# Retention keys turned by VectorE and through DRAM, and a head's states and outputs placed one pair of products later

## The chip, the core and the metric

The kernel runs on one core of a Trainium2 chip. The metric is the device time of one execution in microseconds (us). Engines: PE is TensorE (PEld its weight loads), DVE is VectorE, ACT is ScalarE, POOL is GpSimd, SP is SyncE, which here only issues DMAs.

## The reference

One layer of a hybrid encoder on 512 tokens of width 2048. A projection of the normalized input is split into a sparse attention, a retention with 8 heads of width 128, and gates. The part that is changed is the retention's chunkwise form. Per head, with `rq` and `rk` rotated:

```python
scores = jnp.einsum('bnqhd,bnkhd->bnhqk', qc, kc) * intra_decay
intra = jnp.einsum('bnhqk,bnkhe->bnqhe', scores, vc)
kv = jnp.einsum('bnkhd,bnkhe->nbhde', kc * to_end[:, :, None], vc)
...
cross = jnp.einsum('bnqhd,nbhde->bnqhe', qc * from_start[:, :, None], prev)
y = (intra + cross).reshape(B, L, R_HEADS, R_VAL_DIM)
```

`kv` contracts over tokens, so the keys, which leave the projection with channels on partitions, are needed with tokens on partitions.

## The kernel before

The order of every engine's instructions is written out by hand. A clock of program steps (`step`, one for two matmuls in a pair of products) runs `later(n, f)` jobs n steps after they were asked for. What an engine does is in program order; it waits on semaphores where data or buffers are not ready.

`gemm_pair` computes two 128-column blocks of a projection with seven half-size products. Its 14 runs of 8 matmuls go to the banks v p v p q r q r p p v v p p, a run with `wh` (the high part of a weight) or with `wl` (the low part). It has seven units of weights, 0 to 6, from four loaded tiles `wraw`, called t, w11, w21 and w22 here. ACT makes `wh` from `wraw` (L156), DVE makes `wl` (L161). Unit 4 is tile t after POOL has added another block of weights to it with an accumulating DMA (`add_block`, L119), which POOL issues when DVE has made unit 0's `wl`. Unit 4's `wh` waits for the landing of that DMA. SP loads a pair's tiles (L132) while the pair before it is in the program, as buffers come free, in order.

Three pairs make one head of the retention: the pair of its queries and keys, and two pairs of gates, called **pair A** and **pair B** here. `rotate(1, ...)` is called when the first has ended, and the numbers in `steps` count from there: 0 to 56 lie in A, 56 to 112 in B, 112 to 168 in the next head's pair of queries and keys. Before, all matmuls of a head's retention lie in A: the scores at step 24 (L927) and right behind them three transposes of the keys on PE (L938, into `ps_t`), which ACT copies with the factor `dect[:, 256]` into `kn` (step 29, L941); the states `ps_kv` at 39 (L947), ACT's copy and DVE's recurrence of them (L950, L953), and the outputs `ps_y` at 51 (L962, L964). DVE then normalizes them, turns them in 32x32 blocks (`back`, L990), and SP places the blocks through four DMAs into DRAM (`yd`, L994). B ends with the first use of the next pair. `kn` is the stationary operand of `ps_kv`: PE loads it as weights.

Of the kernel before, what the change touches and what calls it, by code (L numbers as in the profile page):

```python
# [20 lines left out]
NH = 8  # L21
# [14 lines left out]
def block_kernel(tc, xT, pT, posb, posq, w_in, w_v, w_r0, w_r1, w_ik, w_a, w_b, w_o, w_ple, w_gate,  # L36
# [4 lines left out]
    with contextlib.ExitStack() as ctx:  # L41
# [10 lines left out]
        def U(name, dt=F32):  # L52
            return up.tile([128, L], dt, name=name, tag="u")
# [4 lines left out]
        def P(name):  # L58
            return pp.tile([128, L], F32, name=name, tag="p")
# [831 lines left out]

        yd, bd, zd, qd, kd = (dp.tile([NH, 128, L], F32, name=n) for n in ("yd", "bd", "zd", "qd", "kd"))
        vd = dp.tile([2, 7, 128, L], F32, name="vd")

        def retention(h):

            hc = slice(128 * (h % 4), 128 * (h % 4) + 128)
            g128 = (1.0 - 2.0 ** (-5.0 - h)) ** 128
            dect, rv = U("dect"), U("rvh")
            later(24, lambda: sp.dma_start(dect[:, 0:257], dec[:, h, :]))  # L900
            later(32, lambda: sp.dma_start(rv.rearrange("p (t c) -> p t c", t=NT),
                                           rd[h // 4, :, :, hc].rearrange("t p c -> p t c")))
            ct, st = R["ct"], R["st"]
            E = {}

            def rotate(i, o):
                E[i] = o
                b = U("rb")
                act.activation(b[0:64, :], o[64:128, :], AF.Copy)
                act.activation(b[64:128, :], o[0:64, :], AF.Copy)  # L910
                later(3, lambda: dve.tensor_mul(o, o, ct))
                later(5, lambda: dve.tensor_mul(b, b, st))
                later(7, lambda: dve.tensor_add(o, o, b))
                if i:
                    for n, f in steps:
                        later(n, f)

            def queries():
                E["qt"] = U("qt")
                dve.tensor_mul(E["qt"][:, 0:384].rearrange("p (t q) -> p t q", t=3),  # L920
                               E[0][:, 128:].rearrange("p (t q) -> p t q", t=3),
                               dect[:, None, 128:256].to_broadcast([128, 3, 128]))

            def scores():
                ps = E["ps"] = P("ps_rs")
                for t in range(NT):
                    pe.matmul(ps[:, tok(t)], E[1][:, tok(t)], E[0][:, tok(t)], start=True, stop=True)  # L927

            def decay():
                at = E["at"] = U("at")  # L930
                dve.tensor_mul(at.rearrange("p (t q) -> p t q", t=NT), E["ps"].rearrange("p (t q) -> p t q", t=NT),
                               dect[:, None, 0:128].to_broadcast([128, NT, 128]))

            def keys(i):
                if i == 0:
                    ps = E["pk"] = P("ps_t")
                    for t in range(3):
                        pe.transpose(ps[:, tok(t)], E[1][:, tok(t)], ident)  # L938
                else:
                    E["kn"] = U("kn")  # L940
                    act.activation(E["kn"][:, 0:384], E["pk"][:, 0:384], AF.Copy, scale=dect[:, 256:257])  # L941

            def states(i):
                if i == 0:
                    ps = E["ps"] = P("ps_kv")
                    for t in range(3):
                        pe.matmul(ps[:, tok(t)], E["kn"][:, tok(t)], rv[:, tok(t)], start=True, stop=True)  # L947
                elif i == 1:
                    E["s"] = U("state")
                    act.activation(E["s"][:, 0:128], E["ps"][:, 0:128], AF.Copy)  # L950
                else:
                    for t in (1, 2):
                        dve.scalar_tensor_tensor(E["s"][:, tok(t)], E["s"][:, tok(t - 1)], g128, E["ps"][:, tok(t)],  # L953
                                                 op0=OP.mult, op1=OP.add)

            def values_out(t):
                if t == 0:
                    E["py"] = P("ps_y")
                    E["st"] = S("gst", 24)
                    E["mv"] = S("gmv", 8)  # L960
                o = E["py"][:, tok(t)]
                pe.matmul(o, E["at"][:, tok(t)], rv[:, tok(t)], start=True, stop=(t == 0))  # L962
                if t:
                    pe.matmul(o, E["qt"][:, tok(t - 1)], E["s"][:, tok(t - 1)], start=False, stop=True)  # L964

            def norm():
                st, mv, py = E["st"], E["mv"], E["py"]
                for t in range(NT):
                    dve.bn_stats(st[:, 6 * t:6 * t + 6], py[:, tok(t)])
                for t in range(NT):  # L970
                    dve.bn_aggr(mv[:, 2 * t:2 * t + 2], st[:, 6 * t:6 * t + 6])
                rs = S("grs", 4)
                dve.tensor_scalar(rs, mv.rearrange("p (t c) -> p t c", c=2)[:, :, 1], EPS, None, op0=OP.add)
                pool.tensor_tensor(rs, rs, mhalf[:, 0:NT], op=OP.pow)
                E["rs"] = rs

            def scale():
                mv, rs = E["mv"], E["rs"]
                yn = U("yn")
                for t in range(NT):  # L980
                    dve.tensor_scalar(yn[:, tok(t)], E["py"][:, tok(t)], mv[:, 2 * t:2 * t + 1], rs[:, t:t + 1],
                                      op0=OP.subtract, op1=OP.mult)
                E["yn"] = yn

            def back(i):


                if i == 0:
                    E["yb"] = U("yb")
                    dve.transpose(out=E["yb"].rearrange("p (j t c) -> p t j c", j=4, t=4),  # L990
                                  in_=E["yn"].rearrange("p (t j c) -> p t j c", t=4, j=4))
                else:
                    i -= 1
                    sp.dma_start(yd[h].rearrange("(j r) (i x) -> i r j x", j=4, i=4)[i],  # L994
                                 E["yb"][32 * i:32 * i + 32, :].rearrange("r (j x) -> r j x", j=4))

            steps = [(9, queries), (24, scores), (24, lambda: keys(0)), (28, decay), (29, lambda: keys(1))]
            steps += [(n, lambda i=i: states(i)) for i, n in enumerate((39, 41, 43))]
            steps += [(51, lambda t=t: values_out(t)) for t in range(NT)]
            steps += [(57, norm), (70, scale), (90, lambda: back(0))]  # L1000
            steps += [(126 + 2 * i, lambda i=i: back(i)) for i in range(1, 5)]
            return rotate

        x_wanted = collections.deque(x_away)
# [627 lines left out]
X_AWAY = 4  # L1632
X_BACK = (4, 6, 8, 10, 12, 14, 22, 24, 26, 28, 30, 32)
HEAD = 13
WARM = 10
MANUAL = True

# [98 lines left out]
```

## Time and profile before

| | |
|---|---|
| time, median of 3 runs | 1652.87 us (1652.41 to 1652.98) |
| time of the profiled execution | 1653.05 us |
| its span, first to last instruction | 1651.3 us |
| PE busy | 1642.4 us, 99% of the span |
| DVE, ACT, POOL busy | 1310.3, 961.7, 232.7 us |
| chain that ended last, by engine | PE 96%, DVE 2%, ACT 1% |
| retention heads | scores of head 0 at 293.1 us, of head 7 at 726.8 us |

The profiled execution took 1.75 us more than its span, for what lies before the first and after the last instruction. The chain is the work that ended last, followed back from the end: a thing that isn't on it may become slower until it meets it.

### The profile page before, as it was taken

What the parts mean: (1) busy time and instruction counts of PE and PEld (TensorE: products, weight loads), DVE (VectorE), ACT (ScalarE), POOL (GpSimd) and SP (SyncE); (2) the same over time, 40 slices, a digit from 0 to 9 for tenths busy, and PEclk for the clock granted to TensorE, in tenths of its full rate; (3) what the DMA queues carried; (4) which work ended last, traced back from release to release, by engine and by line L of the source; (5) the groups of instructions that cost most, each with busy time, mean ns of one, the idle gap of its engine ahead of it and who ended that gap; (6) DMA issues with size and microseconds to landing.
All of it is one profiled execution on the core that took longest, in us unless ns stands there. A gap on an engine that the chain in (4) does not pass through costs nothing.

```text
span 1651.3 us, 25215 instructions
## 1 busy us (share of the span) xinstructions
PE 1642.4 (99%) x9302; PEld 1444.7 (87%) x9302; DVE 1310.3 (79%) x2030; ACT 961.7 (58%) x1481; POOL 232.7 (14%) x257
## 2 busy tenths in 40 slices
PE   9999999999999999999999999999999999999998
PEld 8998888888888888888888888888888888888997
DVE  8788879888988888877766766787768877888884
ACT  7556545555555555657777765566644444576653
POOL 3100112111111111112331122100000111100111
PEclk9999999999999999999999999999999999999999
DMA  8427999788788788789988888997566788765973
GB/s 311 118 88 236 323 260 277 193 208 223 192 209 216 191 209 220 195 206 248 259 230 228 214 234 219 244 386 272 178 205 180 188 220 226 206 216 146 246 234 134
DMA packets 132987, 362.70 MB, mean 220 GB/s; under 512 B 15936, under 2 KB 28736, under 8 KB 132864
## 3 DMA queue, kind: packets, MB, share of 16 engines
q1 hardware_dynamic: 92608, 239.78, 42.1%
q0 software_dynamic: 27440, 98.32, 32.1%
q10 hardware_dynamic: 12816, 23.00, 3.8%
q8 instruction: 73, 1.20, 0.3%
q14 instruction: 50, 0.41, 0.1%
HBM read 313.32 MB, written 47.71 MB: 219 GB/s over the span
## 4 chain that ended last, share of the span: by engine, by line
PE 96%; DVE 2%; ACT 1%; issue 0%; DVEq 0%; ACTq 0%
PE ps_p L326 26%; PE ps_v L326 17%; PE ps_q L326 9%; PE ps_r L326 9%; PE ps_w L233 3%; PE ps_w L232 3%; PE ps_w L234 3%; PE ps_vn L881 2%; PE ps_vn L879 2%; PE ps_vn L880 2%; PE ps_iq L234 1%; PE ps_iq L232 1%; PE ps_iq L233 1%; PE ps_pg L233 1%; PE ps_pg L232 1%; PE ps_pg L234 1%
## 5 line engine op out<-in xcount | busy, mean ns | idle before, releaser
L161 DVE TENSOR_TENSOR wl<-wraw,wh 128x1024 fp32r<-128x1024 f32 (+3 forms) x472 | 568.4, 1216 | 149.6 <-ACT wh L156 147.2
L156 ACT ACTIVATE wh<-wraw 128x1024 fp32r<-128x1024 f32 (+3 forms) x471 | 486.7, 1041 | 238.5 <-DVE wraw L163 114.6
L119 POOL DMA_DIRECT2D wraw<-w_in x120 | 106.3, 965 | 571.2 <-DVE wl L161 392.1
L326 PE MATMUL ps_p<-hs,wh 128*128 128x512 f32 x640 | 161.0, 393 | 0.0
L265 ACT ACTIVATE e<-ps_p 128x512 f32<-128x512 f32 x152 | 90.3, 594 | 117.3 <-PE ps_p L326 114.9
L326 PEld LDWEIGHTS ps_p<-hs,wh 128*128 128x128 f32 x640 | 115.0, 189 | 20.6
L326 PE MATMUL ps_p<-hs,wl 128*128 128x256 f32 x640 | 89.9, 283 | 0.0
L326 PEld LDWEIGHTS ps_p<-hs,wl 128*128 128x128 f32 x640 | 82.5, 192 | 0.1
L326 PE MATMUL ps_q<-ha,wh 128*128 128x512 f32 x320 | 80.8, 394 | 0.0
L326 PE MATMUL ps_v<-ha,wh 128*128 128x512 f32 x320 | 80.0, 392 | 0.0
L326 PE MATMUL ps_r<-hs,wh 128*128 128x512 f32 x320 | 79.0, 389 | 0.0
L326 PE MATMUL ps_v<-hs,wh 128*128 128x512 f32 x320 | 79.0, 389 | 0.0
L326 PE MATMUL ps_p<-ha,wh 128*128 128x512 f32 x320 | 79.0, 389 | 0.0
L800 ACT ACTIVATE mk<-relf,thr 128x512 f16<-128x512 f32 (+3 forms) x128 | 66.7, 555 | 16.5 <-DVE go L1101 12.0
L1101 DVE TENSOR_TENSOR go<-e_t 128x256 f32<-128x256 f32 x160 | 68.2, 426 | 6.1 <-issue 0.4
L326 PEld LDWEIGHTS ps_r<-hs,wh 128*128 128x128 f32 x320 | 60.1, 188 | 12.5
L326 PEld LDWEIGHTS ps_v<-hs,wh 128*128 128x128 f32 x320 | 60.1, 188 | 12.5
L326 PEld LDWEIGHTS ps_p<-ha,wh 128*128 128x128 f32 x320 | 60.1, 188 | 12.5
L119 POOL DMA_DIRECT2D wraw<-w_o x24 | 21.1, 938 | 348.6 <-DVE t L356 191.4
L326 PEld LDWEIGHTS ps_v<-ha,wh 128*128 128x128 f32 x320 | 59.5, 188 | 12.1
L269 DVE TENSOR_TENSOR e_t<-ps_p,pv 128x512 f32<-128x512 f32 x48 | 33.1, 690 | 45.4 <-ACT e L265 45.2
L326 PEld LDWEIGHTS ps_q<-ha,wh 128*128 128x128 f32 x320 | 57.5, 189 | 12.1 <-issue 1.3
(479 smaller groups left out, 3806.6 us busy)
## 6 DMA issues: line engine op xcount, KB each, us to landing
wraw<-w_in SPq DMA_DIRECT2D x170, 512.0 KB, 5.1
wraw<-w_in POOLq DMA_DIRECT2D x120, 512.0 KB, 8.2
wraw<-w_o SPq DMA_DIRECT2D x32, 512.0 KB, 5.0
wraw<-w_o POOLq DMA_DIRECT2D x24, 512.0 KB, 7.4
wraw<-w_gate SPq DMA_DIRECT2D x24, 512.0 KB, 4.9
wraw<-w_v SPq DMA_DIRECT2D x16, 512.0 KB, 8.7
wraw<-w_b SPq DMA_DIRECT2D x16, 512.0 KB, 5.6
wraw<-w_a SPq DMA_DIRECT2D x16, 512.0 KB, 3.8
```

The costliest lines, as they stand in the source:

```text
L119: pool.dma_start(out=view(raw_tiles[r], nk, cols), in_=src[:, k0:k0 + nk, :], accum_op=OP.add)
L156: act.activation(h, raw, AF.Copy)
L161: dve.tensor_sub(l, raw, h.bitcast(F32))
L232: pe.matmul(o, h[:, k, w], a, start=(s == order[0]), stop=False)
L233: pe.matmul(o, h[:, k, w], b, start=False, stop=False)
L234: pe.matmul(o, l[:, k, w], a, start=False, stop=(s == order[-1]))
L265: act.activation(E[n], src, AF.Copy)
L269: f(t, x, y)
L326: pe.matmul(o[:, co], w[:, k], src, start=(n < 4 and begin and k == 0 and j == 0), stop=(ended[n] == 16), skip_group_check=True)
L800: act.activation(bias_e[b][i // per][:, ln * (i % per):ln * (i % per + 1)], relf[:, :ln], AF.Sign, bias=thr[:, q:q + 1])
L879: pe.matmul(o, a[:, tok(t)], h[:, k], start=(s == 0), stop=False)
L1101: dve.tensor_add(o[:, q], c0, c1)
```

## The change

The three transposes on PE and their PSUM bank go. DVE turns the keys in 32x32 blocks into `kb` (step 29), SP sends them with four DMAs into a new DRAM tile `krd` (steps 32 to 33) and loads it back as `kr` (step 46), and ACT makes `kn` from `kr` at step 75, with the factor from a small copy `te`. The states move from steps 39, 41 and 43 to 77, 79 and 81, the outputs from 51 to 83, their normalization and turning with them. The head's values `rvh` are loaded at step 40, behind the sends, and no longer before pair A.

```diff
+        krd = dp.tile([NH, 128, 384], F32, name="krd")
+
+        def blocks(b, src, n):
+            w = 32 * n
+            dve.transpose(out=b[:, 0:4 * w].rearrange("p (j t c) -> p t j c", j=4, t=n),
+                          in_=src[:, 0:4 * w].rearrange("p (t j c) -> p t j c", t=n, j=4))
+
+        def send(dst, b, i):
+            sp.dma_start(dst.rearrange("(j r) (i x) -> i r j x", j=4, i=4)[i],
+                         b[32 * i:32 * i + 32, 0:dst.shape[1]].rearrange("r (j x) -> r j x", j=4))
...
-            later(32, lambda: sp.dma_start(rv.rearrange("p (t c) -> p t c", t=NT),
-                                           rd[h // 4, :, :, hc].rearrange("t p c -> p t c")))
...
+            def own_values():
+                rv = E["rv"] = U("rvh")
+                sp.dma_start(rv.rearrange("p (t c) -> p t c", t=NT), rd[h // 4, :, :, hc].rearrange("t p c -> p t c"))
...
+                E["te"] = S("tend", 4)[:, 0:1]
+                dve.tensor_copy(E["te"], dect[:, 256:257])
 
             def keys(i):
                 if i == 0:
-                    ps = E["pk"] = P("ps_t")
-                    for t in range(3):
-                        pe.transpose(ps[:, tok(t)], E[1][:, tok(t)], ident)
+                    E["kb"] = U("kb")
+                    blocks(E["kb"], E[1], 3)
+                elif i < 5:
+                    send(krd[h], E["kb"], i - 1)
+                elif i == 5:
+                    E["kr"] = U("kr")
+                    sp.dma_start(E["kr"][:, 0:384], krd[h])
                 else:
                     E["kn"] = U("kn")
-                    act.activation(E["kn"][:, 0:384], E["pk"][:, 0:384], AF.Copy, scale=dect[:, 256:257])
+                    act.activation(E["kn"][:, 0:384].rearrange("p (t i c) -> p i t c", t=3, i=4),
+                                   E["kr"][:, 0:384].rearrange("p (i t c) -> p i t c", i=4, t=3),
+                                   AF.Copy, scale=E["te"])
...
-            steps = [(9, queries), (24, scores), (24, lambda: keys(0)), (28, decay), (29, lambda: keys(1))]
-            steps += [(n, lambda i=i: states(i)) for i, n in enumerate((39, 41, 43))]
-            steps += [(51, lambda t=t: values_out(t)) for t in range(NT)]
-            steps += [(57, norm), (70, scale), (90, lambda: back(0))]
-            steps += [(126 + 2 * i, lambda i=i: back(i)) for i in range(1, 5)]
+            steps = [(9, queries), (24, scores), (28, decay), (40, own_values)]
+            steps += [(n, lambda i=i: keys(i)) for i, n in enumerate(KEYS_AT)]
+            steps += [(n, lambda i=i: states(i)) for i, n in enumerate(STATES_AT)]
+            steps += [(OUT_AT[0], lambda t=t: values_out(t)) for t in range(NT)]
+            steps += [(OUT_AT[1], norm), (OUT_AT[2], scale)]
+            steps += [(n, lambda i=i: back(i)) for i, n in enumerate(OUT_AT[3:])]
...
+KEYS_AT = (29, 32, 32, 33, 33, 46, 75)
+STATES_AT = (77, 79, 81)
+OUT_AT = (83, 87, 94, 105, 128, 130, 132, 134)
```

On ACT, before, `kn` of head 1 stands in pair A, between the `wh` of units 5 and 6 (`pv` and the `e` tiles are copies of finished PSUM banks):

```order
L265 ACTIVATE pv<-ps_v 128x512
L265 ACTIVATE e_3633<-ps_p 128x512
L156 ACTIVATE wh<-wraw 128x1024 x2
L941 ACTIVATE kn<-ps_t,dect 128x384
L156 ACTIVATE wh<-wraw 128x1024
```

After the change it stands in pair B:

```order
L265 ACTIVATE pv<-ps_v 128x512
L265 ACTIVATE e_3844<-ps_p 128x512
L156 ACTIVATE wh<-wraw 128x1024
L959 ACTIVATE kn<-kr,tend 128x4x3x32
L970 ACTIVATE state<-ps_kv 128x128
L156 ACTIVATE wh<-wraw 128x1024 x2
```

The `wh` just ahead of `kn` is that of unit 4 of pair B, and `kn` has moved behind it.

On SP, before, one head's DMAs stand in this order (the last tile of pair A, then the values, then the tiles of two and three quarters pairs, then the outputs):

```order
L900 DMA dect<-dec 128x257
L132 DMA wraw<-w_in 128x1024
L901 DMA rvh<-rd 128x4x128
L132 DMA wraw<-w_in 128x1024 x11
L994 DMA yd<-yb 32x4x128 x4
```

After it:

```order
L910 DMA dect<-dec 128x257
L132 DMA wraw<-w_in 128x1024 x5
L902 DMA krd<-kb 32x4x96 x4
L916 DMA rvh<-rd 128x4x128
L956 DMA kr<-krd 128x384
L132 DMA wraw<-w_in 128x1024 x7
L902 DMA yd<-yb 32x4x128 x4
```

The sends, the values and the load of `kr` now stand ahead of the tiles that are loaded in pair B's part of the program.

On DVE, before, pair A of head 1 goes on like this behind the scores' decay (`at`; MAX and MATCH_REPLACE are a round of the attention's top-k, which runs in the background):

```order
L931 TENSOR_TENSOR at<-ps_rs,dect 128x512
L161 TENSOR_TENSOR wl<-wraw,wh 128x1024
L776 MAX m_3692<-isc 128x8
L777 MATCH_REPLACE isc<-m_3692,isc 128x256
L161 TENSOR_TENSOR wl<-wraw,wh 128x1024 x2
L953 SCALAR_TENSOR_TENSOR state<-state,ps_kv 128x128 x2
```

After it:

```order
L943 TENSOR_TENSOR at<-ps_rs,dect 128x512
L946 COPY tend<-dect 128x1
L161 TENSOR_TENSOR wl<-wraw,wh 128x1024
L898 STREAM_TRANSPOSE kb<-go 128x3x4x32
L776 MAX m_3695<-isc 128x8
L777 MATCH_REPLACE isc<-m_3695,isc 128x256
L161 TENSOR_TENSOR wl<-wraw,wh 128x1024 x2
L269 TENSOR_TENSOR e_t<-ps_v,e_3726 128x512
```

The small copy and the turning of the keys have come ahead of the last `wl`, that of unit 0 of pair B, and the states have left.

## Rows read from the trace of the kernel before

**Rows 1.** The page's chain that ended last, by engine.

```profile
PE 96%; DVE 2%; ACT 1%; issue 0%; DVEq 0%; ACTq 0%
```

**Rows 2.** The chain in order of time, head 1, pair A: start us, us, what.

```profile
355.14 0.89 PE ps_rs L927 x8
356.03 0.33 PE ps_t L938 x3
...
360.82 0.67 PE ps_kv L947 x6
...
365.26 0.45 PE ps_y L962 x4
365.70 0.22 PE ps_y L964 x2
```

**Rows 3.** View by tile, whole span: count, duration ns min/median/max, first and last start.

```profile
L938 PE MATMUL ps_t<-cs,go x24: 272/273/273, 294.0 to 727.9; 128*128 128x128 f32 x24
L941 ACT ACTIVATE kn<-ps_t,dect x8: 557/564/566, 297.2 to 729.8; 128x384 f32<-128x384 f32 x8
L990 DVE STREAM_TRANSPOSE yb<-yn x8: 701/704/705, 322.0 to 755.1; 128x512 f32<-128x512 f32 x8
L973 DVE TENSOR_SCALAR grs<-gmv x8: 169/170/172, 311.9 to 745.6; 128x4 f32<-128x4 f32 x8
```

**Rows 4.** Timeline of head 1, pairs A and B: start us, us, engine, instruction.

```profile
359.30 0.68 DVE L931 TENSOR_TENSOR at<-ps_rs,dect 128x512 f32<-128x512 f32 x1
359.90 1.21 DVE L161 TENSOR_TENSOR wl<-wraw,wh 128x1024 fp32r<-128x1024 f32 x1
...
361.95 2.36 DVE L161 TENSOR_TENSOR wl<-wraw,wh 128x1024 fp32r<-128x1024 f32 x2
...
364.72 0.88 POOL L119 DMA_DIRECT2D wraw<-w_in  x1 [17.32 <-DVE state L953]
...
369.34 0.69 DVE L269 TENSOR_TENSOR e_t<-ps_p,pv 128x512 f32<-128x512 f32 x1 [2.31 <-ACT e L265]
...
374.25 0.60 ACT L265 ACTIVATE e<-ps_p 128x512 f32<-128x512 f32 x1
374.74 1.05 ACT L156 ACTIVATE wh<-wraw 128x1024 fp32r<-128x1024 f32 x1
...
375.67 1.77 PEld L326 LDWEIGHTS ps_r<-hs,wh 128*128 128x128 f32 x8
```

**Rows 5.** Timeline of SP, head 1: first tile load of pair B's part.

```profile
358.35 0.33 SPq L132 DMA_DIRECT2D wraw<-w_in  x1
```

**Rows 6.** Single accumulating DMAs of POOL (L119), by tile: issue, and time to landing.

```profile
L119 POOL DMA_DIRECT2D wraw<-w_in x1: 883/883/883, 364.7 to 364.7; - x1
...
DMA to landing us min/median/max: 8.4/8.4/8.4
...
L119 POOL DMA_DIRECT2D wraw<-w_in x1: 875/875/875, 549.8 to 549.8; - x1
...
DMA to landing us min/median/max: 6.4/6.4/6.4
...
L119 POOL DMA_DIRECT2D wraw<-w_gate x1: 865/865/865, 1528.4 to 1528.4; - x1
...
DMA to landing us min/median/max: 9.2/9.2/9.2
...
L119 POOL DMA_DIRECT2D wraw<-w_o x1: 872/872/872, 1332.1 to 1332.1; - x1
...
DMA to landing us min/median/max: 5.5/5.5/5.5
```

**Rows 7.** SP's loads at 1525.4 to 1526.7 us, by tile: count, issue, landing.

```profile
L132 SPq DMA_DIRECT2D wraw<-w_gate x3: 371/450/672, 1525.4 to 1526.7; - x3
...
DMA to landing us min/median/max: 5.6/7.3/10.0
```

**Rows 8.** DMA issues, 280 to 760 us: count, KB each, median us to landing.

```profile
yd<-yb SPq DMA_DIRECT2D x32, 64.0 KB, 4.7
dect<-dec SPq DMA_DIRECT2D x7, 128.5 KB, 7.4
```

**Rows 9.** Windows: busy time of PE, PEld, DVE, ACT, POOL, PEclk, DMA share, GB/s.

```profile
368.00:375.00 7.00, 7.00 (x40) 6.07 (x40) 5.56 (x15) 4.48 (x7) 2.14 (x3) 1.00 0.99 200
```

**Rows 10.** The chain in order of time, head 4: start us, us, what.

```profile
540.86 0.89 PE ps_rs L927 x8
```

More of the change, by code (lines that the diff above doesn't have):

```diff
@@ L898, in retention @@
             g128 = (1.0 - 2.0 ** (-5.0 - h)) ** 128
-            dect, rv = U("dect"), U("rvh")
+            dect = U("dect")
             later(24, lambda: sp.dma_start(dect[:, 0:257], dec[:, h, :]))
-            later(32, lambda: sp.dma_start(rv.rearrange("p (t c) -> p t c", t=NT),
-                                           rd[h // 4, :, :, hc].rearrange("t p c -> p t c")))
             ct, st = R["ct"], R["st"]
             E = {}
+            def own_values():
+                rv = E["rv"] = U("rvh")
+                sp.dma_start(rv.rearrange("p (t c) -> p t c", t=NT), rd[h // 4, :, :, hc].rearrange("t p c -> p t c"))
             def rotate(i, o):
@@ L946, in states @@
                     for t in range(3):
-                        pe.matmul(ps[:, tok(t)], E["kn"][:, tok(t)], rv[:, tok(t)], start=True, stop=True)
+                        pe.matmul(ps[:, tok(t)], E["kn"][:, tok(t)], E["rv"][:, tok(t)], start=True, stop=True)
                 elif i == 1:
@@ L961, in values_out @@
                 o = E["py"][:, tok(t)]
-                pe.matmul(o, E["at"][:, tok(t)], rv[:, tok(t)], start=True, stop=(t == 0))
+                pe.matmul(o, E["at"][:, tok(t)], E["rv"][:, tok(t)], start=True, stop=(t == 0))
                 if t:
@@ L989, in back @@
                     E["yb"] = U("yb")
-                    dve.transpose(out=E["yb"].rearrange("p (j t c) -> p t j c", j=4, t=4),
-                                  in_=E["yn"].rearrange("p (t j c) -> p t j c", t=4, j=4))
-                else:
-                    i -= 1
-                    sp.dma_start(yd[h].rearrange("(j r) (i x) -> i r j x", j=4, i=4)[i],
-                                 E["yb"][32 * i:32 * i + 32, :].rearrange("r (j x) -> r j x", j=4))
-            steps = [(9, queries), (24, scores), (24, lambda: keys(0)), (28, decay), (29, lambda: keys(1))]
-            steps += [(n, lambda i=i: states(i)) for i, n in enumerate((39, 41, 43))]
-            steps += [(51, lambda t=t: values_out(t)) for t in range(NT)]
-            steps += [(57, norm), (70, scale), (90, lambda: back(0))]
-            steps += [(126 + 2 * i, lambda i=i: back(i)) for i in range(1, 5)]
+                    blocks(E["yb"], E["yn"], NT)
+                else:
+                    send(yd[h], E["yb"], i - 1)
+            steps = [(9, queries), (24, scores), (28, decay), (40, own_values)]
[4 more added lines that the diff above has]
+            steps += [(n, lambda i=i: back(i)) for i, n in enumerate(OUT_AT[3:])]
             return rotate
```

## The prediction

> **What bounds the kernel now.** I read the page's chain first: 96% of what ended last is PE [rows 1]. So an instruction taken off PE is worth its own step on the chain, and anything else counts only where it makes PE wait. Next I read the chain in order of time through one head, to see what the keys cost PE: three transposes take 0.33 us between the scores and the next run, and the states and the outputs have no gap ahead of them [rows 2]. Then the timeline around the places where states and outputs will stand, for ACT, DVE, POOL and SP [rows 4, 5], because there an order is changed that had no waits. Last the landing times of the DMAs that end there [rows 6 to 8].
>
> **Removed from PE.** 24 transposes, three for each of 8 heads [rows 3]. One lasts 273 ns, but they overlap; on the chain three of them advance PE by 0.33 us [rows 2]. 8 x 0.33 = 2.64 us. The scores stay as a block of their own, so no other change between kinds of matmuls is saved.
>
> **Added to DVE.** The turning of the outputs, four blocks of 128 columns, takes 704 ns [rows 3]; three blocks should take 3/4 of that, 0.53 us. The small copy is an operation that the trace doesn't have; between nothing and the 0.17 us of the four-column operation [rows 3] I take 0.1. DVE stood idle for 2.31 us at the end of pair A of head 1 [rows 4], so as DVE time these 0.6 us cost nothing: that idle time hides them, and without it they would cost at most 8 x 0.63 = 5 us. But they come ahead of something that POOL waits for (below). ACT's `kn` only moves. From SBUF and with a permuted read it isn't in the trace; I keep its 0.56 us [rows 3]. If it took the 0.60 us of a 512-column copy [rows 4], that would add 0.04 us to a wait.
>
> **Added to DMA.** Per head four sends of 48 KB, one load of 192 KB, in SP's queue, 3 MB in all. Issuing costs no computing engine anything. What counts is what stands behind them: SP issues in order, and the tiles of pair B's part of the program come after the load of `kr`. The first of these went out at 358.35 [rows 5], while `kb` isn't ready before 359.30 + 0.68 + 0.1 + 1.21 + 0.53 = 361.8 in the same head, and `kr` then waits for the sends to land. So three loads of 512 KB go out several us later than before. Their own users are a pair away; what they do to others is the next paragraph's matter.
>
> **Moved on PE, and what becomes late.** The states (0.67) and outputs (0.45 + 5 x 0.22 = 1.55) leave pair A [rows 2], and the transposes too, so pair B starts 0.33 + 0.67 + 1.55 = 2.55 us earlier after the scores. Inside B nothing is faster: the same work comes back there. But B's first half is now due 2.55 us earlier against everything that was timed by pair A. The tightest of these is unit 4's `wh`. ACT did it at 374.74, right behind the copy `e` at 374.25 [rows 4], so it was not waiting for data. Now it could start at 372.2. Its tile must have received POOL's accumulating DMA, which is issued when DVE's second `wl` of the pair has ended (361.95 + 2.36 = 364.31, issue at 364.72) and landed 8.4 us later [rows 4, 6], at 373.1: before, 1.6 us early; now 0.9 us late, and with DVE's 0.6 us 1.5 us late.
>
> That would harm nobody yet, since PE uses unit 4 only after the rest of `r` and `q`. But `kn` now stands right behind this `wh` on ACT, and PE wants `kn` in the middle of the first `r` run of pair B. The weight loads of that run began at 375.67 [rows 4]; half a run of 1.77 us later and 2.55 us earlier is 374.0. From the landing to `kn` ACT needs 1.05 + 0.56 = 1.61 us, so the DMA has to land by 372.4. In head 1 it lands at 364.72 + 0.6 + 8.4 = 373.7, and PE waits 1.3 us. In head 4 the scores are 540.86 - 355.14 = 185.7 us later [rows 2, 10], so it must land by 558.1; it was issued at 549.8 [rows 6], say 0.3 later now, and at its 6.4 us it lands at 556.5, in time.
>
> How long will this DMA take? Before, SP's queue was empty soon after its issue; now the values, `kr` and three tiles are issued within the same two us. During POOL's DMAs the DMA engines are already 0.99 busy, at 200 GB/s [rows 9]. The bounds: 5.5 us with nothing issued beside it, 9.2 us right behind three such loads of SP [rows 6, 7]. At the old landing times head 1 pays 1.3 and head 4 nothing, 0.65 on average, 5.2 us for eight heads. At 9.2 us head 1 pays 2.1 and head 4 1.2, 13.2 us. At 5.5 nobody pays. The row at 9.2 is nearest in kind (three loads of the same size), the old ones in place; I take the middle of 5.2 and 13.2, 9.2 us.
>
> **The sum.** The profiled execution took 1653.05 us, 0.18 more than the median. 1653.05 - 2.64 + 9.2 = 1659.6, against the median 1659.4. With the two bounds 1655.4 and 1663.4.
>
> After such a wait states and outputs move back together: between them stand ACT's copy and DVE's recurrence, and the same half run and `q` run of PE. POOL's power for the normalization is later too, and has the rest of B. I put nothing down for them.
>
> **Rival one, hidden: the DMA lands by 372.4 in head 1**, that is within 7.1 us of its issue at 365.3. For it: SP's late queue means that no tile load is in flight when POOL issues, and 5.5 us has been seen [rows 6]. Against it: those loads aren't gone, they follow at once. Then only the transposes are left: 1653.05 - 2.64 = 1650.4, 1650.2 against the median. That is 0.16% faster; about 0.2% (3.3 us) is what a measurement of this kernel can tell from no change, so this ends as no change. Above 7.1 us it decides the other way for heads like head 1.
>
> **Rival two, `kr` is what comes late.** `kb` at 361.8; the fourth send some 1.3 us behind at three more issues of 0.4 (as SP's issues at 1525.4 show [rows 7]), 363.1; a turned output landed after 4.7 us, `dect`, the nearest in size to `kr`, after 7.4 [rows 8]. That is 375.2, where 373.4 is due (374.0 less `kn`'s 0.56): 1.8 us a head, 14.4 in all, 1664.6 against the median. For it: two DMAs in a row with a wait between. Against it: the 4.7 us were taken behind tile loads, and the 7.4 us among POOL's DMAs, which come later here.
>
> **Rival three, the two queues share in full.** 512 KB at 200 GB/s are 2.6 us [rows 9]; if SP's loads take every second turn throughout, each add lasts that much longer, 11.0 us in head 1 and 9.0 in head 4. Waits 3.9 and 1.0, 19.6 in all: 1669.8. The Trainium skill (DMA: Bandwidth & Descriptors, Queues, rings and completion order) states the rule: each DMA engine goes round-robin between the queues that it has work for, a packet at a time. No row here shows the turns; the 5.6 to 10.0 us of SP's loads and the 9.2 us of POOL's at 1528.4 agree with sharing, and are less than it in full.
>
> **Rival four, more is gained than the transposes.** It needs 0.7 us beyond 2.64, from handovers or waits that the chain hides: 1649.3. I found no row for it.
>
> That the change doesn't do what it says is no rival: the order shows the transposes gone.
>
> **How the numbers follow.** Forecast, `kn` behind a late add: 0.48 (0.13 of it with small waits, below 1656.2, which is the bound of no change). Rival one 0.22, two 0.18, three 0.07, four 0.05. So faster 0.05; same 0.13 + 0.22 = 0.35; slower 0.35 + 0.18 + 0.07 = 0.60. Likeliest 1659.4; its own range 1655 to 1664. The range for 8 in 10 leaves out rival four and three and most of the upper part of two, and takes in rival one: 1650 to 1667.
>
> **What would show it.** PE's three-transpose rows gone, PE's work 2.6 us less. In the heads a wait of PE's weight loads for ACT's `kn`, near 1 to 2 us, larger in heads like 1 (where a top-k round stands ahead of DVE's `wl`) than in heads like 4; ACT idle ahead of unit 4's `wh`, released by a DMA of POOL. If ACT waits at `kn` itself, for `kr`, rival two is right. If PE has no wait at all, the landing was the step that failed, and the time is near 1650. The forecast is wrong too if DVE's recurrence of the states comes too late for the outputs, which I put at nothing.

## Result and profile after

The changed kernel takes 1665.1 us (median of 6 runs, 1663.79 to 1669.79) against 1652.84 before (6 runs, 1652.41 to 1653.36): a ratio of 1.008, interval 1.0065 to 1.0095. It is slower by 12.3 us. Forecast were 1659.4 and a range of 1650 to 1667. The profiled execution took 1663.79, with a span of 1662.0 us against 1651.3, so what follows explains 10.7 us.

The waits of PE's weight loads in the eight heads of the changed kernel (280 to 790 us), by what they waited for: us in total, times, longest.

```profile
PEld ps_kv L967 <- ACT kn L959: 10.8, 8, 4.0
PEld ps_p L326 <- ACT wh L156: 1.1, 2, 0.7
PEld ps_r L326 <- ACT wh L156: 1.0, 1, 1.0
```

The matmuls themselves (weight loads run ahead of them) stood idle for 7.4 us there:

```profile
PE ps_kv L967 <- ACT kn L959: 7.4, 8, 3.5
```

PE now waits for `kn` at the states in all eight heads. The timeline of head 1 (start us, us, engine, instruction, idle time ahead and what ended it), engine by engine, from the rows that answer to [rows 4, 5]:

```profile
360.75 0.68 DVE L943 TENSOR_TENSOR at<-ps_rs,dect 128x512 f32<-128x512 f32 x1
361.35 0.14 DVE L946 COPY tend<-dect 128x1 f32<-128x1 f32 x1
361.41 1.21 DVE L161 TENSOR_TENSOR wl<-wraw,wh 128x1024 fp32r<-128x1024 f32 x1
362.54 0.57 DVE L898 STREAM_TRANSPOSE kb<-go 128x384 f32<-128x384 f32 x1
...
363.86 2.35 DVE L161 TENSOR_TENSOR wl<-wraw,wh 128x1024 fp32r<-128x1024 f32 x2
366.62 0.88 POOL L119 DMA_DIRECT2D wraw<-w_in  x1 [17.78 <-DVE wl L161]
363.14 1.75 SPq L902 DMA_DIRECT2D krd<-kb  x4
364.94 0.43 SPq L916 DMA_DIRECT2D rvh<-rd  x1
366.25 0.34 SPq L956 DMA_DIRECT2D kr<-krd  x1
366.63 18.11 SPq L132 DMA_DIRECT2D wraw<-w_in  x7
373.83 0.60 ACT L265 ACTIVATE e<-ps_p 128x512 f32<-128x512 f32 x1
375.18 1.06 ACT L156 ACTIVATE wh<-wraw 128x1024 fp32r<-128x1024 f32 x1 [0.75 <-DMA wraw<-w_in]
376.14 0.60 ACT L959 ACTIVATE kn<-kr,tend 128x384 f32<-128x384 f32 x1
376.79 0.94 PE L967 MATMUL ps_kv<-rvh,kn 128*128 128x128 f32 x6 [0.26 <-ACT kn L959]
```

In this head it is the forecast's mechanism, row for row. SP's first tile load of pair B's part goes out at 366.63, with the scores at 356.41: 10.2 us behind them, where it was 358.35 - 354.98 = 3.4 (the timeline before has the scores at 354.98, the chain of [rows 2] 0.16 us later). ACT stands idle for 0.75 us ahead of unit 4's `wh`, for a DMA: POOL's add, issued at 366.62 and landed 8.5 us later. `kn` follows directly, and PE has waited. The add's issue and landing in heads 1 and 5, as [rows 6] show for before:

```profile
L119 POOL DMA_DIRECT2D wraw<-w_in x1: 883/883/883, 366.6 to 366.6; - x1
...
DMA to landing us min/median/max: 8.5/8.5/8.5
...
L119 POOL DMA_DIRECT2D wraw<-w_in x1: 865/865/865, 617.2 to 617.2; - x1
...
DMA to landing us min/median/max: 10.8/10.8/10.8
```

Head 5 is the costly one. Its add takes 10.8 us, PE stands still for 3.5 us, and afterwards the granted clock falls. Windows (busy time of PE, PEld, DVE, ACT, POOL; then PEclk, DMA share, GB/s):

```profile
622.00:626.00 4.00, 4.00 (x24) 3.29 (x22) 2.16 (x2) 2.50 (x4) 0.86 (x1) 1.00 1.05 290
626.00:630.00 4.00, 0.47 (x4) 0.34 (x4) 0.86 (x1) 1.56 (x2) 0.00 (x0) 1.00 1.05 264
630.00:634.00 4.00, 4.00 (x21) 3.70 (x20) 3.46 (x9) 2.29 (x3) 0.00 (x0) 0.61 1.07 272
634.00:638.00 4.00, 4.00 (x32) 3.91 (x32) 3.93 (x13) 0.00 (x0) 0.55 (x1) 0.97 0.57 199
```

At 0.61 and 0.97 of full speed these 8 us do 1.7 us less work than at 1.00. Scores to scores, heads 4 to 6, as [rows 2, 10] have it for before (61.9 a head):

```profile
544.75 1.06 PE L939 MATMUL ps_rs<-go 128*128 128x128 f32 x8
606.75 1.06 PE L939 MATMUL ps_rs<-go 128*128 128x128 f32 x8
673.64 1.05 PE L939 MATMUL ps_rs<-go 128*128 128x128 f32 x8
```

62.0 us for head 4, 66.9 for head 5, the 3.5 and the 1.7 among them. Set against 61.59 us, a head without a wait in a later run (early_a_rv), heads 0 to 6 lose 12.4 us and head 7 some 0.9; less the 2.6 of the transposes that is the 10.7 of the span.

**What goes with a long add** is how soon the first tile load follows it. Issue of that load less issue of the add, and the add's time, both from the rows of the eight heads in order of the first:

| head | 5 | 1 | 7 | 3 | 6 | 4 | 0 | 2 |
|---|---|---|---|---|---|---|---|---|
| load after add, us | -0.6 | 0.0 | 0.2 | 0.8 | 0.9 | 0.9 | 1.4 | 3.1 |
| add, us | 10.8 | 8.5 | 9.6 | 8.9 | 7.5 | 7.5 | 6.5 | 6.7 |

Head 5 is the only one in which tile loads (two) went out ahead of the add. The first experiment below (kn_first) issues its DMAs at nearly the same places and repeats it: 9.5 to 10.7 us at -0.6 to 0.2 (heads 5, 1 and 7), 6.5 to 7.7 at 0.8 to 1.4 (the others).

**Whose wait it is.** Not every one is the add's. Read head by head, ACT stood idle for the add ahead of unit 4's `wh` in heads 1, 3, 5 and 7 (PE idle there 0.3, 0.5, 3.5, 0.6, together 4.9 us), for `kr` in head 2 alone (0.9), and for nothing in heads 0, 4 and 6 (0.4, 0.2, 1.1): there the add had landed, and ACT itself was still at the copies of pair A's end. By weight loads the 10.8 us are 6.6 in the four heads of the add, 1.3 in head 2 and 2.9 in heads 0, 4 and 6.

### The profile page after: what moved, and what is told of

The parts are those of the page before. It is cut to its first block, busy times and chain, and to the rows that moved or that the text cites. A ratio compares the mean times of both kernels' runs of the same rounds, so it can differ in the third digit from the quotient of the medians.

```text
span 1662.0 us, 25245 instructions
## 1 busy us (share of the span) xinstructions
PE 1644.3 (99%) x9278; PEld 1443.4 (87%) x9278; DVE 1316.2 (79%) x2046; ACT 963.0 (58%) x1481; POOL 233.2 (14%) x257
## 4 chain that ended last, share of the span: by engine, by line
PE 50%; DVE 2%; ACT 1%; issue 1%; DMA 1%; DVEq 0%; ACTq 0%; POOLq 0%
PE ps_p L326 14%; PE ps_v L326 10%; PE ps_q L326 5%; PE ps_r L326 5%; PE ps_w L233 3%; PE ps_w L232 3%; PE ps_w L234 3%; PE ps_pg L234 1%; PE ps_pg L233 1%; PE ps_pg L232 1%; PE ps_pg L1538 1%; PE ps_pg L1539 1%; PE ps_pg L1540 1%; DMA wraw<-w_in 1%; PE ps_bias L813 1%
## 5 line engine op out<-in xcount | busy, mean ns | idle before, releaser
L119 POOL DMA_DIRECT2D wraw<-w_in x120 | 106.4, 950 | 567.9 <-DVE wl L161 471.0
L326 PEld LDWEIGHTS ps_v<-ha,wh 128*128 128x128 f32 x320 | 60.1, 188 | 12.5
L326 PEld LDWEIGHTS ps_v<-hs,wh 128*128 128x128 f32 x320 | 60.1, 188 | 12.5
L326 PEld LDWEIGHTS ps_p<-ha,wh 128*128 128x128 f32 x320 | 60.1, 188 | 12.5
L119 POOL DMA_DIRECT2D wraw<-w_o x24 | 21.1, 942 | 348.5 <-DVE t L356 191.5
L163 DVE TENSOR_TENSOR wraw<-wraw 128x1024 f32<-128x1024 f32 x52 | 63.7, 1225 | 1.8
```

The costliest lines, as they stand in the source:

```text
L119: pool.dma_start(out=view(raw_tiles[r], nk, cols), in_=src[:, k0:k0 + nk, :], accum_op=OP.add)
L163: dve.tensor_add(raw, raw, view(raw_tiles[plus], nk, cols))
L326: pe.matmul(o[:, co], w[:, k], src, start=(n < 4 and begin and k == 0 and j == 0), stop=(ended[n] == 16), skip_group_check=True)
```

## The experiments

All are edits of the changed kernel; times are set against the kernel before on the same chip. The changed kernel's own ratio is the 1.008 above.

**`kn` ahead of the `wh`** (kn_first). One number: the place of `kn` on ACT.

```diff
-KEYS_AT = (29, 32, 32, 33, 33, 46, 75)
+KEYS_AT = (29, 32, 32, 33, 33, 46, 71)
```

> Only the place of `kn` on ACT changes: two rows earlier, ahead of the last copy `e` of pair A and of unit 4's `wh`. Theory one (`kn` was late because it stood behind the `wh` that waits for POOL's add): the waits of PE at ps_kv, 10.8 us by weight loads in the changed kernel, fall to about 1.5 us, which is head 2, where `kr` landed 20.08 us after the scores; 1652.84 - 2.64 for the transposes + 1.5 + some 2.5 of waits in other pairs = 1654, at most 1657. Theory two (`kr` itself is what comes late): ACT now waits at `kn` for `kr` in most heads, PE's wait stays above 7 us, time 1662 or more. Theory three (`e` behind `kn` now holds a bank that PE wants): waits of PE for ACT's `e` appear, about 0.6 us a head, 1659.

1662.76 us, ratio 1.0058 (1.0041 to 1.0074). The waits of weight loads in the heads:

```profile
PEld ps_y L984 <- DVE state L973: 6.0, 4, 3.2
PEld ps_r L326 <- ACT wh L156: 1.1, 3, 0.5
```

No row for ps_kv is left, and no wait of ACT for `kr` shows (in heads 0, 2 and 3 it landed just 0.02 to 0.03 us ahead of `kn`): so the wait at ps_kv did come from the place behind the `wh`. But the time hardly fell, and theory one's number was wrong by 9 us. The state copy, the next link from PE back to PE, is also ACT's, and it stands behind the same `wh`. ACT's timeline of head 1 there:

```profile
373.71 0.61 ACT L959 ACTIVATE kn<-kr,tend 128x384 f32<-128x384 f32 x1
374.22 0.59 ACT L265 ACTIVATE e<-ps_p 128x512 f32<-128x512 f32 x1
377.38 1.06 ACT L156 ACTIVATE wh<-wraw 128x1024 fp32r<-128x1024 f32 x1 [2.58 <-DMA wraw<-w_in]
378.35 0.26 ACT L970 ACTIVATE state<-ps_kv 128x128 f32<-128x128 f32 x1
```

PE starts ps_kv at 376.39 and has its result some 1.1 us before 378.35. The late add now holds the outputs in place of the states; in head 5 it again took 10.7 us, and the clock fell again (0.50 in the window 632 to 636 us).

**States later** (states_later).

```diff
-STATES_AT = (77, 79, 81)
-OUT_AT = (83, 87, 94, 105, 128, 130, 132, 134)
+STATES_AT = (84, 86, 88)
+OUT_AT = (91, 95, 102, 113, 136, 138, 140, 142)
```

> The transposed keys are as in the changed kernel; states stand 7 steps later (84, 86, 88) and outputs 8 (91), some 2.8 us more of PE's work ahead of ps_kv. Theory one (a handover that was due too early): only a head with an add like head 5's (3.5 us of wait) still waits, under 1 us; waits at ps_kv under 1.5 us in all, what is left is the transposes' gain and the other pairs' waits: 1652.84 - 2.64 + 1 + 2.5 = 1653.7. Theory two (the wait is set by the whole queue and moves along, since every later tile is late too): PE waits elsewhere for as much, 1662 or more. If the state copy, now behind unit 5's `wh` on ACT, is late, the outputs wait for `state`: 0.5 to 1 us a head, 1658 to 1662.

1668.37 us, ratio 1.0094 (1.0079 to 1.0109): no faster than the changed kernel, and 15 us above theory one.

```profile
PEld ps_r L326 <- ACT wh L156: 7.7, 4, 2.3
PEld ps_y L984 <- DVE state L973: 4.2, 5, 1.7
PEld ps_kv L967 <- ACT kn L959: 1.4, 1, 1.4
```

The waits for `kn` fell as expected, to head 5's alone. In their place came waits for the state copy, and a new one in the pair of products behind pair B. It comes from a neighbour of the later place and from a late add together: DVE's scaling of the outputs now stands ahead of pair B's last results, behind a `wl` that waited 4.99 us for ACT's `wh`. DVE's timeline, head 0:

```profile
325.95 1.22 DVE L161 TENSOR_TENSOR wl<-wraw,wh 128x1024 fp32r<-128x1024 f32 x1 [4.99 <-ACT wh L156]
327.09 1.36 DVE L1001 TENSOR_SCALAR yn<-ps_y,gmv,grs 128x128 f32<-128x128 f32 x4
328.37 0.68 DVE L269 TENSOR_TENSOR e_t<-ps_v,e 128x512 f32<-128x512 f32 x1
```

ACT's `go` waits for these results, and the next pair's `wh` stands behind that. The `wh` for which DVE waited had itself waited 3.23 us for another of POOL's adds, which took 10.1 us. In the changed kernel the `wh` at this place waits as long (3.32 us), but DVE has scaled the outputs before it. So theory two has a part in this: late tiles hold the pairs behind as well, and its 1662 or more came true.

**The move alone** (move_only). Transposes on PE and `kn` behind them as before the change; states, outputs and the values' load as after it.

```diff
                 if i == 0:
-                    E["kb"] = U("kb")
-                    blocks(E["kb"], E[1], 3)
...
+                    ps = E["pk"] = P("ps_t")
+                    for t in range(3):
+                        pe.transpose(ps[:, tok(t)], E[1][:, tok(t)], ident)
                 else:
                     E["kn"] = U("kn")
+                    act.activation(E["kn"][:, 0:384], E["pk"][:, 0:384], AF.Copy, scale=E["te"])
...
-KEYS_AT = (29, 32, 32, 33, 33, 46, 75)
+KEYS_AT = (24, 29)
```

> The transposes stay on PE and `kn` right behind them on ACT (step 29), nothing goes through DRAM; only states, outputs and the values' load stand where the changed kernel has them. Theory one (the place itself is free, the wait belongs to where `kn` stands): no wait at ps_kv, PE's work as before: 1652.8, between 1651.5 and 1654.5. Rival (the second half of the move costs: state copy, recurrence or POOL's power late, or tiles late because pair A is shorter and pair B is due earlier): waits of PE for `state`, ps_y or for tiles in pair B, 1656 or more.

1654.31 us, ratio 1.0007 (0.9998 to 1.0017). The only new wait of note:

```profile
PEld ps_y L978 <- DVE state L967: 1.1, 2, 0.8
```

So the place by itself costs about 1 us, by the state copy, and that can't be told from no change.

**Without the way through DRAM** (no_dram). `kn` is read from `kb` at its place; sends and `kr` are gone, and with them the gathering of the blocks across partitions, which this version leaves out.

```diff
-                elif i < 5:
-                    send(krd[h], E["kb"], i - 1)
-                elif i == 5:
-                    E["kr"] = U("kr")
-                    sp.dma_start(E["kr"][:, 0:384], krd[h])
...
-                                   E["kr"][:, 0:384].rearrange("p (i t c) -> p i t c", i=4, t=3),
+                                   E["kb"][:, 0:384].rearrange("p (i t c) -> p i t c", i=4, t=3),
...
-KEYS_AT = (29, 32, 32, 33, 33, 46, 75)
+KEYS_AT = (29, 75)
```

> The sends and the load of `kr` are left out and `kn` is read from `kb` at its place (the blocks then aren't gathered across partitions, so this part of the computation is left out); everything else stands as in the changed kernel, `kn` behind unit 4's `wh`. Theory one, contention (pair B's tile loads, held up in SP's queue behind the sends and `kr`, are what makes POOL's add land late): loads go out at +3 to +8 us after the scores again, the add lands as before the change (by +17.3), PE's wait at ps_kv falls from 10.8 to about 3 us, and the waits in the pairs behind it (2.5 us) go: 1652.84 - 2.64 + 3 = 1653. Rival (the order on ACT alone, with the add issued later behind DVE's new blocks, makes the wait): it stays near 9 us, 1659 to 1661.

1654.61 us, ratio 1.001 (1.0001 to 1.0019): 10.5 us of the changed kernel's time are gone.

```profile
PEld ps_kv L962 <- ACT kn L954: 4.2, 6, 1.5
```

Head 1's add there, by tile:

```profile
L119 POOL DMA_DIRECT2D wraw<-w_in x1: 881/881/881, 366.4 to 366.4; - x1
...
DMA to landing us min/median/max: 6.7/6.7/6.7
```

The eight adds for unit 4 take 5.6 to 8.5 us here, 7.2 in the mean; before the change 6.4 to 8.4, 7.3; in the changed kernel 6.5 to 10.8, 8.2. So with SP's queue free the adds are as before, and 4.2 us of waits still stay. 0.8 of them are in heads 2 and 3, where ACT waited 0.4 and 0.3 us for the add; 3.5 are in heads 0, 4, 5 and 6, where ACT waited for no DMA. The largest is head 6's, in which ACT's only idle time behind that `go` is 0.40 us, in which it issues a DMA of its own:

```profile
681.27 0.63 ACT L1123 ACTIVATE go<-go 128x512 f32<-128x512 f32 x1 [1.33 <-DVE go L1114]
...
682.30 0.72 ACT L800 ACTIVATE mk<-relf,thr 128x512 f16<-128x512 f32 x1 [0.40 <-ACT go L1123]
682.93 1.04 ACT L156 ACTIVATE wh<-wraw 128x1024 fp32r<-128x1024 f32 x1
...
684.97 0.58 ACT L265 ACTIVATE e<-ps_p 128x512 f32<-128x512 f32 x1
685.45 1.05 ACT L156 ACTIVATE wh<-wraw 128x1024 fp32r<-128x1024 f32 x1
686.39 0.61 ACT L954 ACTIVATE kn<-kb,tend 128x384 f32<-128x384 f32 x1
```

From pair A's last `go` on, ACT works through a row that ends in `kn`, and that row alone is too long there.

**Without DRAM and `kn` first** (no_dram_first). The edit above, with 71 in the place of 75.

> Leaves out the DRAM round trip as the run without it (the keys' blocks aren't gathered across partitions, so this part of the computation is left out), and puts `kn` two rows earlier on ACT, ahead of `e` and unit 4's `wh`. Theory one (the losses add up from separate handovers: the queue, `kn` behind the `wh`, and the state copy behind the same `wh`): waits at ps_kv of 4.2 us without the DRAM part go, waits for `state` stay at what the move alone showed, 1.1 us; so 1654.3 of the move alone less 2.64 for the transposes, 1651.7, between 1650.8 and 1653. Rival (the wait for the add only moves on to `state`, as it did with the DRAM part in): 4 us for `state`, 1654.5.

1653.88 us, ratio 1.0005 (0.9996 to 1.0015). Again ps_kv's wait went and one for `state` came, 2.5 us where theory one had 1.1 and the rival 4: by the time the rival is the nearer of the two. The wait of 4.2 us is passed on in part, not removed.

**Loads first** (loads_first). Sends behind the first tile load, `kr` behind the second.

```diff
-KEYS_AT = (29, 32, 32, 33, 33, 46, 75)
+KEYS_AT = (29, 58, 58, 59, 59, 64, 75)
```

> As the changed kernel, but in SP's queue the sends stand behind the first tile load of pair B's part and `kr` behind the second. Theory one (late tile loads make the add late): the first load goes out at +3 us again, the others 2 us earlier than in the changed kernel; the add lands about a load's 2 us earlier in the heads that waited for it, waits for the add near 5 us; but `kr`, behind two loads of 512 KB, lands at +15 to +20: two or three heads wait for `kr` at `kn` for about 1 us. Waits 7 to 9 us in all at ps_kv, other pairs' waits gone: 1658 to 1660. Rival two of the prediction (`kr`) would show here with more than 10 us of ACT waiting at `kn`: 1664 or more.

1669.07 us, ratio 1.0095 (1.008 to 1.011), 9 us above the expected 1658 to 1660. PE's weight loads waited 14.4 us for `kn`, 8.3 of them in heads 6 and 7, where ACT waited for `kr` itself:

```profile
ACT kn L959 <- DMA kr<-krd: 6.8, 2, 3.7
```

In these two heads `kr` went out 14.0 and 12.5 us after the scores and landed 23.3 and 21.9 us after them. The prediction's rival two becomes real when `kr` is sent behind the tiles. Nor did the adds get shorter (7.5 to 9.8 us, 8.6 in the mean): in heads 1 to 3, where ACT waited longest for them, `kr` and the third tile load now went out 0.3 to 1.0 us behind the add.

**Early sends** (early_b). The turning, the sends and `kr` some 20 steps earlier, ahead of the scores; all else in place.

```diff
-KEYS_AT = (29, 32, 32, 33, 33, 46, 75)
+KEYS_AT = (8, 9, 9, 10, 10, 22, 75)
```

> The turning stands some 20 steps earlier (step 8, right behind the rotation, before the scores), the sends and the load of `kr` with it; `kn`, states and outputs stay where the changed kernel has them. All of the traffic is there, but SP's queue is free again when pair B's tile loads come. Theory one (contention by late tile loads, seen when the DRAM part was left out): loads go out 3 to 8 us after the scores, waits of PE at ps_kv near 4 us as without the DRAM part, time near 1654.6, 1653 to 1656. Rival (3 MB more through the DMA engines cost, wherever they stand): waits of 7 us or more, 1658 or more. New risk: DVE's turning stands ahead of `qt` and of two `wl`; if PE then waits for `wl` in pair A, 0.5 us a head, 1658.

1657.01 us, ratio 1.0027 (1.0015 to 1.0038), a little over the expected 1653 to 1656, and 8 us below the changed kernel.

```profile
PEld ps_kv L967 <- ACT kn L959: 5.1, 5, 1.5
```

The adds take 6.8 to 8.8 us, 8.0 in the mean. So the traffic alone brings the mean from 7.2 back up, but no add takes 10.8, and PE's wait is near the 4.2 without any traffic. So the adds above 8.8 us go with the held-up tile loads and not with the 3 MB by themselves. 2.4 us more than without the way through DRAM are left; 1.0 us of waits of weight loads for `wl`, behind DVE's earlier turning, is new.

**Early sends, states back in pair A** (early_a, early_a2, early_a_rv, early_a_rv2, early_a_wl). With the keys in SBUF early, nothing forces the move.

```diff
-KEYS_AT = (29, 32, 32, 33, 33, 46, 75)
-STATES_AT = (77, 79, 81)
-OUT_AT = (83, 87, 94, 105, 128, 130, 132, 134)
+KEYS_AT = (8, 9, 9, 10, 10, 22, 40)
+STATES_AT = (46, 48, 50)
+OUT_AT = (56, 62, 75, 95, 126, 128, 130, 132)
...
-            steps = [(9, queries), (24, scores), (28, decay), (40, own_values)]
+            steps = [(9, queries), (24, scores), (28, decay), (32, own_values)]
```

> Turned keys and early sends as in the run with the early sends, but `kn` at step 40, states at 46 to 50 and outputs at 56, in pair A, and the values' load back at 32: the transposes are gone and no handover stands in pair B. Theory one (the loss is all from the handovers in pair B and from SP's queue): no waits at ps_kv or ps_y over 1 us in all, 1653.0 - 2.64 = 1650.4, 1649.5 to 1652. Rival one (`kr`, sent at about -1.5 us and loaded behind a tile load, lands later than +5 us): ACT waits at `kn` for `kr`, PE up to 1 us a head, 1654 to 1658. Rival two (`kn` and the state copy stand behind pair A's `wh` on ACT as they did behind pair B's): PE waits for `kn` or `state` with ACT idle for a tile, 1654 to 1660.

1672.97 us, ratio 1.0124 (1.0108 to 1.0139). Neither theory named the cause: the values' load now stood behind `kr` and two tile loads, and the states wait for it. The timeline of PE and SP in head 1:

```profile
366.21 0.91 PE L967 MATMUL ps_kv<-rvh,kn 128*128 128x128 f32 x6 [1.55 <-DMA rvh<-rd]
360.20 0.42 SPq L916 DMA_DIRECT2D rvh<-rd  x1
```

That load landed after 5.9 us, at 366.1, and ps_kv began 0.1 us later.

A second version had `kn` at 36 and states at 41 to 45, outputs 3 steps earlier, and `kr` at 24, one tile load further back.

> As the run with states at 46, but `kn` at 36, ahead of one copy `e` and one `wh` of ACT, and states at 41 to 45, some 2 us earlier than there. If `kr` lands by +4 us after the scores: 1650.4 as well. If it lands later (rival one of that run), ACT waits at `kn` for it here and PE at ps_kv, about 2 us more a head than with states at 46: 1658 or more. If there the `wh` ahead of `kn` was the holder, this run is the faster of the two.

1674.94 us, ratio 1.0131 (1.0116 to 1.0146); ACT waited for `kr` in seven heads, 14.7 us in all, which is rival one of early_a. But the values' load was as late here too: it landed 7.3 to 9.5 us behind the scores, and ps_kv began 0.13 to 0.14 us behind that landing in every head, with `kn` done at about the same time. The run can't tell what `kr` alone would have cost.

Then early_a with the values' load at step 6, ahead of the sends (`(6, own_values)`):

> As the run with early sends and states at 46 in pair A, where PE waited at ps_kv until the values' load had landed (9.2 to 12.1 us after the scores, ps_kv 0.14 us behind it in every head): only that load moves, from step 32, behind `kr` in SP's queue, to step 6, ahead of the sends. Theory one (the values' load was the holder): the 16.4 us of waits at ps_kv go; `kr` then lands at about +6.5, `kn` runs at +7.0 and PE wants it at +8.0; head 6, where `kn` ran at 8.35, may keep 1 us. 1653.0 - 2.64 + 0 to 1.5 = 1650.4 to 1652. Rival (`kn` and the state copy behind pair A's `wh` on ACT are the next that come late): waits for `kn` or `state` of 0.5 to 1 us a head, 1655 to 1658.

1653.03 us, ratio 0.9999 (0.999 to 1.0007). The waits at ps_kv are gone but for head 6's 0.5 us, as expected; the time is 1 us above the expected range. Scores of heads 4 and 5:

```profile
540.75 1.06 PE L939 MATMUL ps_rs<-go 128*128 128x128 f32 x8
602.34 1.06 PE L939 MATMUL ps_rs<-go 128*128 128x128 f32 x8
```

61.59 us a head without a wait, against 61.91 before [rows 2, 10]: the 0.32 us of the transposes are there. What eats them is small: three waits of weight loads for `wl`, 1.0 us, since DVE's turning now stands ahead of it, and head 6's 0.5. PE's first 20 matmuls, some 7 us, also took 0.7 us longer in this profile, with no edit there; other runs' profiles differ there by as much.

> As the run above, with states at 52 to 56 and outputs at 62, some 2 us later in pair A. If `kn` or `kr` was just late there, this one has no wait left: 1650.4 (1649.5 to 1651.5). If the state copy, now behind pair A's `go` on ACT, or the later outputs hold PE, waits for `state` of 0.5 us a head: 1654. If nothing waited in the run above, the two are the same.

1653.03 us, ratio 0.9998 (0.9989 to 1.0007), the same: head 6's wait is gone, others of 0.7 us appear. The last run kept these states and put the turning behind a `wl`:

```diff
-KEYS_AT = (8, 9, 9, 10, 10, 22, 40)
+KEYS_AT = (16, 17, 17, 18, 18, 26, 43)
```

> As the run with states at 52, but the turning stands one `wl` and `qt` later on DVE (steps 16 to 26 for the turning, sends and load, `kn` at 43), so that DVE's 0.57 us no longer stands ahead of the `wl` for which PE waited 0.4, 0.4 and 0.2 us there. If these waits and the place of the turning are what ate the transposes' 2.64 us: 1653.2 - 2.64 + 0.5 = 1651.1, 1650 to 1652, faster by 0.1%. If `kr`, which starts some 1.3 us later, lands too late for `kn`, ACT waits at `kn` and PE at ps_kv: 1655 or more. If the gain is lost elsewhere than in waits (the lengths of PE's own runs): 1653 again.

1654.55 us, ratio 1.0007 (0.9998 to 1.0016): `kr` came too late in most heads, and PE's weight loads waited 2.5 us for `kn` in four. The view puts 5.1 us of ACT's idle time ahead of `kn` (four heads) down to `kr` and 6.7 (three more) to DVE, but there too `kn` began 0.1 us behind the landing of `kr`. No version beat the kernel before by what a measurement can tell.

## Why the prediction was right, and where it was off

**Side, mechanism and range held**, the range by the median: two of the six runs, 1668.8 and 1669.8, lie above its 1667. The wait stands where the forecast put it: at ps_kv, for `kn`, behind unit 4's `wh`, in four heads behind POOL's add. kn_first shows that the place behind the `wh` makes the wait at ps_kv, no_dram and early_b that SP's late queue makes most of its length. Two terms were right in size. The transposes: 2.64 forecast, 0.32 a head seen, 2.6. The add: the middle between "the old landing times" (6.4 and 8.4) and 9.2 us is some 8.3; it came out at 8.2 in the mean.

**The likeliest time was 5.7 us too low,** and the measured one lies outside the likeliest case's own range of 1655 to 1664. The terms:
- Waits at ps_kv, by weight loads: 10.8 where 9.2 were put down. Near in sum, but by another distribution, so the nearness is luck: 1.3 to 2.1 us were put down for heads like 1 and 0 to 1.2 for heads like 4, and these two waited 0.7 and 0.6. I had read ACT's `wh` at 374.74 as "not waiting for data. Now it could start at 372.2". That step failed: ACT's own row from `go` to `kn` didn't come 2.55 us earlier with pair B. In head 1 `e` began 17.4 us behind the scores, where 372.2 for the `wh` behind it means some 16.7, and in heads 0, 4 and 6 the row was too long whatever the add did. That is 2.9 of the 10.8, and with head 5 it is 3.5 of the 4.2 us that no_dram kept. Head 5's add, 10.8 us, lay above the upper bound of 9.2 and gave 4.0 of the 10.8.
- The clock: put at nothing. After head 5's gap PE ran below full speed, 1.7 us in the profile. The two longest of the six runs, 1668.8 and 1669.8, had a mean granted clock of 0.995 where the others had 0.998 or 0.999, so this also spreads the times: by these rounded clocks 0.003 of 1667 us, an estimate of 5 us, is about what the two are longer by.
- Other waits: nothing was put down, and 2.1 us of weight loads' waits elsewhere are new. The 1.0 at ps_r, in the pair behind pair B, goes with the late queue: no_dram doesn't have it. The 1.1 at ps_p stands at pair A's end in heads 1 and 2, and no_dram has it too. The matmuls' own row there names DVE's `wl`, which comes 0.5 us later behind the turning while pair A's end is due 1.0 us earlier. So the turning did cost PE something, where the forecast had "as DVE time these 0.6 us cost nothing".
- "After such a wait states and outputs move back together" hid something: the state copy is behind the same `wh`. It cost nothing in the changed kernel only because `kn` had already paid. With `kn` ahead of the `wh` it costs 6.0 us (kn_first), and with the queue as before the change 2.5 (no_dram_first) or 1.1 (move_only).
- Together, by weight loads, 10.8 + 2.1 + 1.7 = 14.6 us; by the matmuls' own idle time 7.4 + 1.4 + 1.7 = 10.5. The 13.3 that the heads lost lie between: PE loses 0.1 to 0.2 us less than each wait of its weight loads.

**The rivals.** Rival one (hidden) would have needed both the add and ACT's row in time. Rival two (`kr`) was 0.9 us of PE's idle time in one head, not 14.4: a send to DRAM landed after 1.7 us in the median where 4.7 had been assumed, though `kr` itself took up to 7.5. Rival three, full sharing of the two queues, would have made each add 2.6 us longer; the mean grew by 0.9. The Trainium skill (DMA: Bandwidth & Descriptors, Queues, rings and completion order) states turns between the queues packet by packet. The direction agrees, and so does the table above; no run here shows the turns.

Two slips of the prediction change nothing: rival four's 1649.3 should be 1650.2 - 0.7 = 1649.5, and beside the add of 5.5 us, read as "with nothing issued beside it", POOL issued two more adds of its own (at 1334.8 and 1335.5); only SP issued nothing.

**Open:** why head 1's add, with a load beside it from the start, took 8.5 us here and 10.7 in kn_first. The second tile load followed the add by 1.3 us here and by 0.5 there, which fits, but no run changed that alone. Open too is how much of the spread of the six runs is such an add and how much the clock behind it.

## What to carry to other kernels

Where work moves that goes from PE to another engine and back, list every instruction of that engine's queue ahead of each handover, with what it waits for: here two links of one chain stood behind the same copy, and freeing one only handed the wait to the other. A transfer taken off the compute path still stands in a queue: what it delays there are the loads behind it, so send it where that queue has slack (early_b) before moving the consumer. And check that a gain is larger than the measurement's bound before arranging five engines around it: the best version found here shows the 0.32 us a head and yet can't be told from no change.

## What was not expected of the hardware

- A DMA of 48 KB from SBUF to DRAM landed 1.6 to 1.7 us after its issue in 30 of 32 cases, in the two others after 3.3 and 3.8. `kr`, 192 KB back, took 2.9 to 3.8 us where it went out ahead of POOL's add (heads 1, 5, 7), 6.3 to 7.5 where it went out behind it.
- VectorE's turning of 384 columns took 0.57 us, against 0.70 for 512: more than three quarters, 0.53. A copy of one column took 0.14 us.
- ScalarE's `kn` with a permuted read from SBUF took 0.603 us, against 0.564 from PSUM in order [rows 3].
- After a gap of PE of 3.5 us the granted clock was 0.61 in the next 4 us (a mean of the 2.4 and the 1.2 GHz level), while the gap's own window still showed 1.00; in kn_first, after 2.9 idle us in one window, 0.50 and 0.73 in the two that followed it. So a wait of a few us cost half as much again in the first case (1.7 us of work), and about as much again in the second (some 3 us).
